# The up product of a decoder layer: eight pairs of output tiles by seven products of quarters, and low parts by adding loads

## The chip, the cores and the metric

The kernel runs on one core of one Trainium2 chip. The metric is device time in microseconds for one execution of the program, median of several runs. All arithmetic is on fp32 data. The matrix engine (TensorE, PE in the profile) works on operands rounded to fp32r, so the kernel splits each fp32 matrix into a high part (the rounded value) and a low part (what is left over), and forms each product as three: high by high, high by low, low by high.

## The reference

One decoder layer with 512 tokens (T), width 1024 (D) and feed-forward width 2816. The mixers ahead of the feed-forward part are not touched. What matters here:

```python
def conv_ffn(h, w_up, conv_w, conv_b, w_down):
    up = h @ w_up                              # 512 x 1024 by 1024 x 5632
    padded = jnp.pad(up, ((0, 0), (CONV_WIDTH - 1, 0), (0, 0)))
    conv = conv_b + conv_w[0] * padded[:, 0:T]
    for i in range(1, CONV_WIDTH):
        conv = conv + conv_w[i] * padded[:, i:i + T]
    gate, val = jnp.split(conv, 2, axis=-1)
    return (jax.nn.gelu(gate, approximate=True) * val) @ w_down
...
        h = rmsnorm(x, norm_ffn_pre[l])
        f = conv_ffn(h, ffn_w_up[l], ffn_conv_w[l], ffn_conv_b[l], ffn_w_down[l])
        x = x + rmsnorm(f, norm_ffn_post[l])
```

## The kernel before

**The up product.** The output of `h @ w_up` is kept with channels on the partitions: 44 tiles of 128 channels by 512 tokens, each in one bank of PSUM (the matrix engine's accumulators). They come in 22 pairs (`NF`): tile 2n is the gate and tile 2n+1 the value of pair n. The right operand is `h2h`/`h2l`, the high and low part of the normalised activations: 128 partitions, 8 chunks (`KC`) of the width, 512 tokens. The left operand is one weight tile of 128 x 1024 for each output tile, 512 KB in fp32, which holds 8 chunks of 128 x 128. `up_mm` walks over the 8 chunks, and `mm3` (L110 to L114) issues the three matmuls of a chunk, 128 x 512 each: 24 matmuls a tile, 48 a pair. The first two pairs (`FIRST`) are done in halves of 256 tokens, since their operand is finished in halves. The other 20 run one after the other in the loop over `j`.

**The weights.** `prefetch` goes through a fixed list (`weight_order`) two tiles ahead of use (`AHEAD`). For each tile `load_raw` loads the fp32 weights from HBM into `raw` (two buffers, issued on the SP queue), ScalarE casts them into `whi` (L70), and VectorE subtracts to get `wlo` (L71). `whi` and `wlo` have four buffers each. A buffer is written again only when the last matmul that reads it is done, and an engine works through its own instructions strictly in the program's order.

**Behind each pair.** `up_finish` runs the three taps of the convolution on both tiles (`conv`: one ScalarE activation, L837, and two VectorE operations, L838 and L840, which read PSUM), the gelu on ScalarE (L852) and the product on VectorE. The down product that follows is itself made of seven products of quarters (the list `steps`) in place of eight; its left operands are sums and differences of halves of the activations, which `up_finish` forms at once for each pair of pairs (`y7`, `a2`, `ay`; L864 is one such difference of 128 x 256).

**The down product.** It runs through seven steps of six chunks of weights. The weights of a step are made from those of the step before in the six `chain` buffers: either a plain load on SP, or a load on the POOL queue that adds what it reads to what the buffer holds (`accum_op=ALU.add`, L883). `w_prepare` splits a chunk (L70 and L71 again) and then issues the load for the next step; `l_prepare` splits the left operand of a step, 4 chunks at a time; `q_mm` does the matmuls (128 x 512), and `combine`, `lower_token` and `upper_token` put the steps' results together, normalise and store.

Of the kernel before, what the change touches and what calls it, by code (L numbers as in the profile page):

```python
# [14 lines left out]
P = 128  # L15
# [9 lines left out]
TH = T // 2  # L25
LEVELS = (64, 32, 16, 8, 4, 2, 1)
# [10 lines left out]
def weight_order():  # L37

    o = [("t", T_SK), ("t", T_GQ)] + [("v", k) for k in range(8)]
    o += [("t", T_GQ + 1)] + [("t", T_GK + i) for i in range(2)] + [("t", T_R + i) for i in range(4)]  # L40
    for br in (1, 0, 2):
        for m in range(8):
            if br == 1 and m == 6:
                o += [("t", T_PU + g) for g in range(4)]
            if m % 2 == 0:
                o.append(("b", br, m // 2))
            o.append(("t", T_GATE + GATE_OF[br] * 8 + m))
    o += [("o", k) for k in range(4)] + [("u", i) for i in range(2 * NF)]
    return o
# [3 lines left out]
def kernel(ctx: ExitStack, tc: tile.TileContext, x, xT, w_first, w_tiles, w_v, w_br, w_out, w_up, w_down,  # L53
# [775 lines left out]
    with tc.tile_pool(name="fp", bufs=1) as fp:  # L829
        y7 = fp.tile([P, 2, NH, TH], F32R, tag="y7", name="y7")  # L830
        a2 = fp.tile([P, 2, NH, TH], F32, tag="a2", name="a2")
        ay = fp.tile([P, 4, NH, TH], F32, tag="ay", name="ay")
        ch = [fp.tile([P, 2 * T], F32, tag=f"ch{p}", name=f"chain{p}") for p in range(4)]
        def conv(ps, i, keep=False):
            t0 = (fp.tile([P, T], F32, tag="tk", name="tk", bufs=2) if keep else
                  fp.tile([P, T], F32, tag="t0", name="t0", bufs=3))
# [7 lines left out]
        kept = {}  # L844

        def up_finish(n, pg, pv):


            i = n // 2
            tg = conv(pg, 2 * n, n % 2 == 0)  # L850
            tv = conv(pv, 2 * n + 1)
            nc.scalar.activation(tg, tg, AF.Gelu_apprx_tanh)  # L852
            if n % 2 == 0:
                nc.vector.tensor_mul(tg, tg, tv)
                nc.vector.tensor_sub(tv[:, :TH], tg[:, TH:], tg[:, :TH])
                nc.scalar.copy(y7[:, 0, i, :], tv[:, :TH])
                nc.scalar.copy(ay[:, 2, i, :], tg[:, :TH])
                nc.vector.tensor_sub(y7[:, 1, i, :], tv[:, :TH], y7[:, 0, i, :].bitcast(F32))
                kept[i] = tg
            else:  # L860
                t0 = kept.pop(i)
                nc.vector.tensor_mul(a2[:, :, i, :], tg.rearrange("p (h t) -> p h t", h=2),
                                     tv.rearrange("p (h t) -> p h t", h=2))
                nc.vector.tensor_sub(ay[:, 0, i, :], t0[:, TH:], a2[:, 1, i, :])  # L864
                nc.vector.tensor_sub(ay[:, 1, i, :], t0[:, :TH], ay[:, 0, i, :])
                nc.vector.tensor_sub(ay[:, 3, i, :], a2[:, 0, i, :], ay[:, 1, i, :])
# [3 lines left out]
        steps = ((None, (1, 1), True), (ay[:, 2], (0, 0), False), (ay[:, 0], (0, 1), True), (ay[:, 1], (1, 1), True),  # L870
                 (a2[:, 1], (1, 0), True), (ay[:, 3], (1, 1), False), (a2[:, 0], (1, 0), False))
# [18 lines left out]
        def w_prepare(upto):  # L890
            while len(ready) < min(upto, len(todo)):
                s, p = todo[len(ready)]
                k0, k1 = pairs[p]
                hi, lo = new_w()
# [5 lines left out]
        for i in range(2 * FIRST):  # L900
            up_mm(pf[i], up_first[i], slice(256, 512))
        for j in range(FIRST):
            up_finish(j, pf[2 * j], pf[2 * j + 1])
        for j in range(FIRST, NF):
            pp = []
            for i in (2 * j, 2 * j + 1):
                w = weight("u", i)
                ps = psm.tile([P, T], F32, tag="mm", name=f"up{i}")
                up_mm(ps, w, slice(0, T))
                pp.append(ps)  # L910
            if j == NF - 5:
                for p in range(4):
                    chain_load(0, p)
            if j == NF - 1:
                w_prepare(2)
                ch += [wp.tile([P, 2 * T], F32, tag="raw", name=f"chain{p}", bufs=2) for p in (4, 5)]
                for p in (4, 5):
                    chain_load(0, p)
            up_finish(j, *pp)

        lh = hp.tile([P, 2, 2, 4, TH], F32R, tag="hhi", name="lhs")
        cb = hp.tile([P, 4, 2, T], F32, tag="hlo", name="comb")
        gpost = cb.rearrange("p i b c -> p i (b c)")[:, 3, :]
        nc.gpsimd.dma_start(gpost, g_ffn_post.partition_broadcast(P))
        nc.gpsimd.tensor_scalar(gpost, gpost, -0.5, None, op0=ALU.mult)
        left = {}

        def l_split(s, g):
# [3 lines left out]
            nc.scalar.copy(lh[:, h, 0, :n, :], src)  # L932
            nc.vector.tensor_sub(lh[:, h, 1, :n, :], src, lh[:, h, 0, :n, :].bitcast(F32))
            left[s, g] = h

        lgroups = [(s, g) for s in range(1, len(steps)) for g in range(len(groups))]
# [4 lines left out]

        def lhs(s, k, part, tb):
            tk = slice(tb * P, (tb + 1) * P)
            if s == 0:
                return y7[:, part, k, tk]
            return lh[:, left[s, k // 4], part, k % 4, tk]
# [73 lines left out]
        for s in range(len(steps)):  # L1020
            whole = len(pairs) if s < len(steps) - 1 else 3
            for p in range(whole):
                w_prepare(s * len(pairs) + p + (3 if whole == len(pairs) else 4))
                if p % 2 == 0:
                    l_prepare((s - 1) * len(groups) + p // 2 + 2 if s else 2)
# [103 lines left out]
```

## Time and profile before

| | |
|---|---|
| Time, median of 3 runs | 780.96 us (779.97 to 781.41) |
| The profiled execution's own time | 781.12 us |
| Its span, first to last instruction | 779.3 us |
| Mean granted clock of TensorE | 0.998 of full speed |
| Up product whole tiles, matmuls 128x512 | 960 (three rows of 320, 389 ns mean duration) |
| HBM read, written | 89.84 MB, 2.10 MB |

The page gives one execution. Engines are named PE (TensorE's matmuls), PEld (its weight loads, which overlap the matmuls), DVE (VectorE), ACT (ScalarE), POOL (GpSimd) and SP (which only issues loads and stores here). A duration of a matmul in the trace reaches from its start until its result is written, and matmuls overlap; so their price is read from the distance of their starts and not from their durations. A load is listed with the time from its issue until its last byte has landed. A stretch is given as from:to in us, with busy time and number of instructions of each engine.

### The profile page before, as it was taken

The numbers are of one execution on the slowest core, as the hardware profiler recorded it, in microseconds if no ns is written. First come the engines' busy times: TensorE is split into PE (matmuls) and PEld (weight loads), VectorE is DVE, ScalarE is ACT, GpSimd is POOL, SyncE is SP. The second block draws the span as 40 slices with busy tenths as digits, with TensorE's granted clock in tenths as the row PEclk, the third lists the DMA queues.
The fourth block names the chain that finished last, engine by engine and source line by source line (L and its number), as shares of the span: only waits on it lengthen the run. The fifth ranks groups of instructions, "written<-read, shape, count | busy, mean of one in ns | idle before, by whom it ended". The sixth has DMA issues, their size and how long they took to land.

```text
span 779.3 us, 9734 instructions
## 1 busy us (share of the span) xinstructions
PE 770.3 (99%) x3686; PEld 638.9 (82%) x3686; DVE 514.5 (66%) x784; ACT 356.9 (46%) x583; POOL 55.1 (7%) x70
## 2 busy tenths in 40 slices
PE   9999999999999999999999999999999999999996
PEld 8899776888886888888888988888888888888885
DVE  5564688378696555654648557766666766766896
ACT  6554554482233442423535434434344343565582
POOL 0100000002513000000000100000000000233000
PEclk9999999999999999999999999999999999999999
DMA  8524212122133212232351483322323225499761
GB/s 309 193 89 146 71 57 79 55 85 105 54 104 127 70 66 86 105 102 87 131 221 54 139 211 111 109 108 82 109 84 105 105 84 135 130 185 193 200 212 54
DMA packets 28526, 92.56 MB, mean 119 GB/s; under 512 B 3392, under 2 KB 3664, under 8 KB 28480
## 3 DMA queue, kind: packets, MB, share of 16 engines
q1 hardware_dynamic: 24048, 77.83, 29.0%
q0 software_dynamic: 4288, 14.11, 9.1%
q8 instruction: 29, 0.48, 0.2%
q14 instruction: 17, 0.14, 0.1%
q10 hardware_dynamic: 144, 0.00, 0.0%
HBM read 89.84 MB, written 2.10 MB: 118 GB/s over the span
## 4 chain that ended last, share of the span: by engine, by line
PE 97%; DMA 1%; DVE 1%; ACT 0%; issue 0%; DVEq 0%; ACTq 0%
PE up L113 10%; PE up L112 10%; PE up L114 10%; PE pj L112 9%; PE pj L113 9%; PE pj L114 8%; PE q L962 4%; PE q L963 4%; PE q L964 4%; PE py L112 3%; PE py L114 3%; PE py L113 3%; PE pq L206 3%; PE pz L749 2%; PE pz L751 2%; PE pz L750 2%
## 5 line engine op out<-in xcount | busy, mean ns | idle before, releaser
L71 DVE TENSOR_TENSOR wlo<-raw,whi 128x1024 fp32r<-128x1024 f32 (+1 forms) x105 | 125.3, 1196 | 112.3 <-ACT whi L70 112.3
L70 ACT CAST whi<-raw 128x1024 fp32r<-128x1024 f32 (+1 forms) x105 | 107.5, 1025 | 182.9 <-PE pj L113 89.1
L112 PE MATMUL up<-h_hi,whi 128*128 128x512 f32 (+1 forms) x384 | 143.8, 375 | 0.0
L113 PE MATMUL up<-h_lo,whi 128*128 128x512 f32 (+1 forms) x384 | 142.7, 372 | 0.0
L114 PE MATMUL up<-h_hi,wlo 128*128 128x512 f32 (+1 forms) x384 | 142.5, 371 | 0.0
L112 PE MATMUL pj<-h_hi,whi 128*128 128x512 f32 x296 | 120.5, 407 | 0.0
L113 PE MATMUL pj<-h_lo,whi 128*128 128x512 f32 x296 | 116.1, 392 | 0.0
L114 PE MATMUL pj<-h_hi,wlo 128*128 128x512 f32 x296 | 115.8, 391 | 0.0
L113 PEld LDWEIGHTS up<-h_lo,whi 128*128 128x128 f32 x384 | 72.3, 188 | 12.5
L114 PEld LDWEIGHTS up<-h_hi,wlo 128*128 128x128 f32 x384 | 72.3, 188 | 12.5
L112 PEld LDWEIGHTS up<-h_hi,whi 128*128 128x128 f32 x384 | 72.2, 188 | 12.6
L112 PEld LDWEIGHTS pj<-h_hi,whi 128*128 128x128 f32 x296 | 55.7, 188 | 15.9 <-issue 3.4
L114 PEld LDWEIGHTS pj<-h_hi,wlo 128*128 128x128 f32 x296 | 55.6, 188 | 12.1 <-issue 0.2
L113 PEld LDWEIGHTS pj<-h_lo,whi 128*128 128x128 f32 x296 | 55.8, 188 | 10.5 <-issue 1.0
L71 DVE TENSOR_TENSOR wlo<-chain,whi 128x1024 fp32r<-128x1024 f32 (+1 forms) x42 | 47.3, 1132 | 19.9 <-ACT whi L70 19.9
L70 ACT CAST whi<-chain 128x1024 fp32r<-128x1024 f32 (+1 forms) x42 | 41.1, 981 | 29.6 <-PE q L964 22.8
L883 POOL DMA_DIRECT2D chain<-in_w_down_dram x24 | 21.0, 876 | 438.6 <-ACT tk L837 201.3
L962 PE MATMUL q<-whi,lhs 128*128 128x512 f32 x132 | 51.3, 389 | 0.0
L963 PE MATMUL q<-wlo,lhs 128*128 128x512 f32 x132 | 51.3, 389 | 0.0
L964 PE MATMUL q<-whi,lhs 128*128 128x512 f32 x132 | 51.3, 389 | 0.0
L674 DVE TENSOR_TENSOR g<-pj,rstd_b 128x512 f32<-128x512 f32 x24 | 16.4, 688 | 27.4 <-PE pj L114 27.3
L964 PEld LDWEIGHTS q<-whi,lhs 128*128 128x128 f32 x132 | 24.8, 188 | 5.2
(308 smaller groups left out, 1264.4 us busy)
## 6 DMA issues: line engine op xcount, KB each, us to landing
raw<-in_w_up_dram SPq DMA_DIRECT2D x44, 512.0 KB, 3.2
raw<-in_w_tiles_dram SPq DMA_DIRECT2D x37, 512.0 KB, 3.2
chain<-in_w_down_dram SPq DMA_DIRECT2D x20, 512.0 KB, 4.4
chain<-in_w_down_dram POOLq DMA_DIRECT2D x20, 512.0 KB, 7.5
raw<-in_w_br_dram SPq DMA_DIRECT2D x12, 512.0 KB, 3.3
raw<-in_w_out_dram SPq DMA_DIRECT2D x8, 512.0 KB, 3.2
raw<-in_w_v_dram SPq DMA_DIRECT2D x8, 328.0 KB, 2.9
xT<-in_xT_dram SPq DMA_DIRECT2D x8, 256.0 KB, 5.0
```

The lines of the kernel that those rows point to most:

```text
L70: nc.scalar.copy(hi[:, c], raw[:, c])
L71: nc.vector.tensor_sub(lo[:, c], raw[:, c], hi[:, c].bitcast(F32))
L112: nc.tensor.matmul(ps, lh, rh, start=first, stop=False)
L113: nc.tensor.matmul(ps, lh, rl, start=False, stop=False)
L114: nc.tensor.matmul(ps, ll, rh, start=False, stop=last)
L206: nc.tensor.matmul(pq[i], w[:, kc, i * P : (i + 1) * P], h[:, kc, :], start=kc == 0 and n == 0, stop=kc == KC - 1 and n == 2)
L674: nc.vector.tensor_mul(g1, gates.pop((br, m)), rstd_b)
L749: nc.tensor.matmul(pz[t][n], mh[:, kc % 4, tk], wh[:, ns], start=kc == 0, stop=False)
L883: nc.gpsimd.dma_start(c, w_down[kh, nh, :, k, :], accum_op=ALU.add)
L962: nc.tensor.matmul(ps, hi, wh[:, c], start=k == 0 and not last, stop=False, skip_group_check=last)
L963: nc.tensor.matmul(ps, hi, wl[:, c], start=False, stop=False, skip_group_check=last)
L964: nc.tensor.matmul(ps, lo, wh[:, c], start=False, stop=k == NH - 1, skip_group_check=last)
```

## The change

Pairs n = 5, 7, ..., 19 (`SEVEN`) are computed by seven products of quarters. The weights of such a pair are seen as a 2 x 2 block matrix (two halves of the width, two tiles of channels), the activations as 2 x 2 as well (two halves of the width, two halves of the tokens). Seven products of sums and differences of the quarters, four chunks deep and 256 tokens wide, replace the eight that the plain way amounts to. One product is 4 chunks by 3 terms, 12 matmuls of 128x256 (`part_mm`). `up_seven` interleaves the seven products with the plain pair n+1, whose tiles 2n+2 and 2n+3 are called A and B in the prediction. A "double pair" is the two together; the order of work in it is quarter b11, 2 chunks of A, p3, 3 chunks of A, p2, 3 chunks of A, b21, 2 chunks of B, p1, 3 chunks of B, p4, 3 chunks of B, b22.

Four operands `ys0` to `ys3` are formed once from the activations (`y_steps`, while the pairs 2 to 4 run). The weights' sums are formed for each double pair: `sra` is a plain load of 512 KB, `s1` two plain loads of 256 KB and two adding loads on top (`s_load`, issued at the end of p4's preparation for the next double pair; one buffer), `s2` comes from additions on VectorE. The weight slots become one ring of eight half tiles: a plain tile takes two, a quarter one (`slots`, `place`, `free`). `fill` prepares as far ahead as the ring has room, in the order of use. For plain tiles from number 10 on, the low part is no longer a VectorE subtraction: ScalarE writes `-raw`, rounded like the high part, into the low buffer, and a load on POOL adds the fp32 weights from HBM on top (L939, L940). Results of the seven products are kept as copies of PSUM on ScalarE (`keep`, L1080) and put together on VectorE.

For the down product `up_finish` now stores only products and one difference (`act`); two of the other differences move into `l_split` (steps 3 and 5), step 0's operand is split there too, and the `chain` buffers 0 to 3 take the place of `ys0` and `ys1` once the last double pair is done.

```diff
+SEVEN = (5, 7, 9, 11, 13, 15, 17, 19)
...
-    o += [("o", k) for k in range(4)] + [("u", i) for i in range(2 * NF)]
+    o += [("o", k) for k in range(4)] + [("u", i) for i in range(2 * FIRST)]
...
+        def slots(n):
+            if n == 2 and slot["n"] % 2:
+                slot["n"] += 1
+            i = slot["n"] % 8
+            slot["n"] += n
+            c = slice(i % 2 * T, (i % 2 + n) * T)
+            return wt[i // 2][0][:, c], wt[i // 2][1][:, c]
...
             if n % 2 == 0:
...
+                nc.vector.tensor_sub(act[:, 4, i, :], act[:, 1, i, :], act[:, 0, i, :])
             else:
...
+                nc.vector.tensor_sub(act[:, 1, i, :], act[:, 1, i, :], act[:, 3, i, :])
...
+        def s_load(n):
+            qt["a"] = f4(f"sra{n}", "sra")
+            nc.sync.dma_start(qt["a"], w_up[2 * n])
+            qt["s1"] = f4(f"s1_{n}", "sm1")
+            nc.sync.dma_start(qt["s1"][:, :T], w_up[2 * n, :, :T])
+            nc.sync.dma_start(qt["s1"][:, T:], w_up[2 * n + 1, :, T:])
+            for h in range(2):
+                nc.gpsimd.dma_start(qt["s1"][:, h * T : (h + 1) * T], w_up[2 * n + 1, :, :T], accum_op=ALU.add)
+
+        def half(src):
+            hi, lo = slots(1)
+            nc.scalar.copy(hi, src)
+            nc.vector.tensor_sub(lo, src, hi.bitcast(F32))
+            return hi, lo
+
+        def prep(item):
+            if item[0] == "t":
+                hi, lo = slots(2)
+                raw = load_raw(w_up[item[1]])
+                nc.scalar.copy(hi, raw)
+                if True and item[1] >= 2 * SEVEN[0]:
+                    nc.scalar.activation(lo, raw, AF.Copy, scale=-1.0)
+                    nc.gpsimd.dma_start(lo, w_up[item[1]], accum_op=ALU.add)
+                else:
+                    nc.vector.tensor_sub(lo, raw, hi.bitcast(F32))
+                return hi, lo
...
+            if q == "p2":
+                s2 = qt["s2"] = f4(f"s2_{n}", "sm2")
+                nc.vector.tensor_add(s2[:, :T], a[:, :T], s1[:, T:])
+                return half(s2[:, :T])
...
+            if q == "p4":
+                s2 = qt["s2"]
+                nc.vector.tensor_add(s2[:, T:], s2[:, :T], a[:, T:])
+                r = half(s2[:, T:])
+                later = [m for m in SEVEN if m > n]
+                if later:
+                    s_load(later[0])
+                return r
...
+        def fill():
+            while done["i"] < len(items):
...
+                if at + size - min(place.values(), default=at) > 8 or (it[0] == "s" and not qt):
+                    break
+                place[it] = at
+                got_w[it] = prep(it)
+                done["i"] += 1
...
+            if s == 3:
+                nc.vector.tensor_sub(src, src, act[:, 1, k0:k1, :])
+            if s == 5:
+                nc.vector.tensor_sub(src, act[:, 2, k0:k1, :], act[:, 0, k0:k1, :])
...
+        def part_mm(ps, w, r, first):
+            for kc in range(4):
+                c = slice(kc * P, (kc + 1) * P)
+                terms = ((w[0], r[0]), (w[0], r[1]), (w[1], r[0]))
+                for t, (x, y) in enumerate(terms):
+                    nc.tensor.matmul(ps[:, :TH], x[:, c], y[:, kc, :], start=first and kc == 0 and t == 0,
+                                     stop=kc == 3 and t == 2, skip_group_check=not first)
...
+            b11, p3 = up_weight("s", n, "b11"), up_weight("s", n, "p3")
+            part_mm(bx, b11, hq(0, 0), True)
+            free("s", n, "b11")
+            q1 = keep("q1", bx)
+            wa = up_weight("t", 2 * n + 2)
+            whole_mm(pn[0], wa, range(0, 2))
+            part_mm(by, p3, yq(0), True)
...
```

TensorE where output tile `up19` ends and `up20` begins, before the change: rows of one kind, tile after tile (`whi` and `wlo` are the weight buffers with their running numbers).

```order
L112 MATMUL up19_4371<-h2_hi_3100,whi_4291 128x512
L113 MATMUL up19_4371<-h2_lo_3101,whi_4291 128x512
L114 MATMUL up19_4371<-h2_hi_3100,wlo_4292 128x512
L112 MATMUL up20_4415<-h2_hi_3100,whi_4336 128x512
L113 MATMUL up20_4415<-h2_lo_3101,whi_4336 128x512
L114 MATMUL up20_4415<-h2_hi_3100,wlo_4337 128x512
```

So every low part is read right behind the first two matmuls of its tile.

The same tile of output, `up20`, as tile A of the double pair n = 9, after the change, from the first of its own rows: `uy_9` and `ux_9` are accumulators of the quarter products, `ys0` and `ys1` the new operands.

```order
L113 MATMUL up20_4463<-h2_hi_3100,whi_3670 128x512
L114 MATMUL up20_4463<-h2_lo_3101,whi_3670 128x512
L1059 MATMUL uy_9_4461<-ys0_3672,whi_3668 128x256 x2
L1059 MATMUL uy_9_4461<-ys0_3672,wlo_3669 128x256
L1059 MATMUL uy_9_4461<-ys0_3672,whi_3668 128x256 x2
L1059 MATMUL uy_9_4461<-ys0_3672,wlo_3669 128x256
L1059 MATMUL uy_9_4461<-ys0_3672,whi_3668 128x256 x2
L1059 MATMUL uy_9_4461<-ys0_3672,wlo_3669 128x256
L1059 MATMUL uy_9_4461<-ys0_3672,whi_3668 128x256 x2
L1059 MATMUL uy_9_4461<-ys0_3672,wlo_3669 128x256
L1059 MATMUL ux_9_4460<-ys1_3673,whi_3664 128x256 x2
L1059 MATMUL ux_9_4460<-ys1_3673,wlo_3665 128x256
```

Between the second matmul of `up20` and its third, the one that reads the low part `wlo`, now stand two groups of quarter matmuls: p3's twelve, and six of the twelve of p2, whose first half stands ahead of it in this row.

ScalarE at the same place of the program. Before the change, casts of the weights (L70), starts of the convolution (L837) and gelus (L852) take turns:

```order
L70 CAST whi_4411<-raw_4409 128x1024
L837 ACTIVATE t0_4396<-up18_4340,small_sb_86 128x512
L852 ACTIVATE t0_4396<-t0_4396 128x512
L70 CAST whi_4442<-raw_4440 128x1024
L837 ACTIVATE t0_4400<-up19_4371,small_sb_86 128x512
L70 CAST whi_4487<-raw_4485 128x1024
```

After it, around the preparation of `up20` (its `raw` is number 4414, its slots `whi_3670` and `wlo_3671`, which tile B of the double pair before, `up17`, holds until its last matmul). L929 is a cast of a quarter, L937 that of a plain tile, L939 its negated copy, L1080 a copy out of PSUM, L883 a start of the convolution, L896 a gelu:

```order
L929 CAST whi_3664<-s2_9_4419 128x512
L929 CAST whi_3668<-s2_9_4419 128x512
L929 CAST whi_3664<-sra9_4311 128x512
L883 ACTIVATE t0_4438<-ua_7_4256,small_sb_86 128x512
L937 CAST whi_3670<-raw_4414 128x1024
L939 ACTIVATE wlo_3671<-raw_4414 128x1024
L1115 ACTIVATE ub_7_4257<-ux_7_4251 128x256
L896 ACTIVATE t0_4438<-t0_4438 128x512
L883 ACTIVATE t0_4442<-ub_7_4257,small_sb_86 128x512
L883 ACTIVATE t0_4449<-up16_4254,small_sb_86 128x512
L1080 ACTIVATE q1_4479<-ux_9_4460 128x256
L937 CAST whi_3666<-raw_4481 128x1024
```

All casts of the sums for n = 9 and the convolution's start on the sum `ua_7` now stand ahead of the cast of `up20`'s weights, and the gelu and three more starts of the convolution behind it; the next plain tile's cast (`raw_4481`) is queued behind those.

More of the change, by code (lines that the diff above doesn't have):

```diff
@@ L829 @@
     with tc.tile_pool(name="fp", bufs=1) as fp:
[L830 to L836, printed above, removed]
+        act = fp.tile([P, 5, NH, TH], F32, tag="act", name="act")
@@ new lines, with f4 @@
+        wt = [new_w() for _ in range(4)]
+        slot = {"n": 0}
+        def slots(n):
[5 more added lines that the diff above has]
+            return wt[i // 2][0][:, c], wt[i // 2][1][:, c]
+        def f4(name, tag):
+            return fp.tile([P, 1024], F32, tag=tag, name=name)
+        ys = [fp.tile([P, 2, 4, TH], F32R, tag=f"ys{i}", name=f"ys{i}") for i in range(4)]
@@ new lines, with up_weight @@
+        place = {}
+        def fill():
+            while done["i"] < len(items):
+                it = items[done["i"]]
+                size = 2 if it[0] == "t" else 1
+                at = slot["n"] + (size == 2 and slot["n"] % 2)
+                if at + size - min(place.values(), default=at) > 8 or (it[0] == "s" and not qt):
[3 more added lines that the diff above has]
+                done["i"] += 1
+        def up_weight(*item):
+            assert items[done["taken"]] == item, (items[done["taken"]], item)
+            done["taken"] += 1
+            fill()
+            return got_w[item]
@@ L872, with free @@
+        def free(*item):
+            del place[item]
+        steps = ((act[:, 4], (1, 1), True), (act[:, 0], (0, 0), False), (act[:, 1], (0, 1), True),
+                 (act[:, 0], (1, 1), True), (act[:, 3], (1, 0), True), (act[:, 1], (1, 1), False),
+                 (act[:, 2], (1, 0), False))
         pairs = tuple((k, min(k + 2, NH)) for k in range(0, NH, 2))
@@ L898, in w_prepare @@
                     chain_load(s + 1, p)
[L900 to L925, printed above, removed]
         left = {}
@@ new lines @@
+        for i in range(2 * FIRST):
+            up_mm(pf[i], up_first[i], slice(256, 512))
+        for j in range(FIRST):
+            up_finish(j, pf[2 * j], pf[2 * j + 1])
+        yst = y_steps()
+        n = FIRST
+        while n < NF:
+            if n in SEVEN:
+                us, pn = up_seven(n)
+                up_finish(n, *us)
+                up_finish(n + 1, *pn)
+                n += 2
+                if n - 2 == SEVEN[-1]:
+                    c0 = fp.tile([P, 2, 2 * T], F32, tag="ys0", name="chain01")
+                    c1 = fp.tile([P, 2, 2 * T], F32, tag="ys1", name="chain23")
+                    ch = [c0[:, 0, :], c0[:, 1, :], c1[:, 0, :], c1[:, 1, :]]
+                    for p in range(4):
+                        chain_load(0, p)
+                continue
+            pp = up_std(n)
+            if n == NF - 1:
+                lh = [fp.tile([P, 2, 4, TH], F32R, tag=f"ys{i}", name=f"lhs{i}") for i in (2, 3)]
+                l_prepare(2)
+                w_prepare(2)
+                ch += [wp.tile([P, 2 * T], F32, tag="raw", name=f"chain{p}", bufs=2) for p in (4, 5)]
+                for p in (4, 5):
+                    chain_load(0, p)
+            up_finish(n, *pp)
+            for _ in range(3):
+                next(yst, None)
+            n += 1
+            if n == SEVEN[0] - 1:
+                for _ in yst:
+                    pass
+                s_load(SEVEN[0])
```

137 lines of the change are left out of this document (113 added, 24 removed).

## The prediction, as it was made before the changed kernel was run

> **What bounds the kernel now.** I read the page first, then busy time by stretch, then the matmuls one by one. From the page (span, part 1, and part 4, the chain that ended last):
>
> ```profile
> span 779.3 us, 9734 instructions
> ...
> PE 770.3 (99%) x3686; PEld 638.9 (82%) x3686; DVE 514.5 (66%) x784; ACT 356.9 (46%) x583; POOL 55.1 (7%) x70
> ...
> PE 97%; DMA 1%; DVE 1%; ACT 0%; issue 0%; DVEq 0%; ACTq 0%
> ```
>
> TensorE holds 97% of the chain: a matmul removed is time won, and a pause put into its row is time lost. By stretch (length, then busy us of PE, PEld, DVE, ACT, POOL, granted clock, DMA share, GB/s):
>
> ```profile
> 483.00:657.00 174.00, 174.00 (x769) 144.10 (x768) 114.59 (x155) 72.21 (x97) 1.73 (x2) 1.00 0.30 102
> ...
> 549.00:571.00 22.00, 22.00 (x99) 18.22 (x98) 14.05 (x19) 9.25 (x14) 0.00 (x0) 1.00 0.28 96
> ...
> 683.00:698.00 15.00, 15.00 (x68) 12.43 (x67) 8.86 (x9) 8.59 (x11) 4.85 (x6) 1.00 1.05 189
> 698.00:713.00 15.00, 15.00 (x67) 12.41 (x67) 10.09 (x10) 9.45 (x12) 5.28 (x7) 1.00 1.03 189
> 743.00:758.00 15.00, 15.00 (x68) 12.43 (x67) 15.00 (x28) 12.51 (x21) 0.00 (x0) 1.00 0.68 217
> ```
>
> The first row is exactly 16 of the up pairs, those that become the eight double pairs (a pair of seven products with a plain pair woven in): 768 matmuls in 174.0 us, 0.2266 us each, 10.88 us a pair, without a gap. VectorE and ScalarE are two thirds and two fifths busy there, POOL not at all.
>
> **What is removed.** The trace already has matmuls 256 wide, in the first pairs (start, duration):
>
> ```profile
> 440.45 0.28 PE L114 MATMUL up<-h_hi,wlo 128*128 128x256 f32 x1
> ...
> 443.45 0.28 PE L112 MATMUL up<-h_hi,whi 128*128 128x256 f32 x1
> ...
> 448.49 0.19 PEld L113 LDWEIGHTS up<-h_lo,whi 128*128 128x128 f32 x1
> ```
>
> From the first start to the last are 25 steps: 0.120 us each, though each has its own weight load of 0.19 us, which overlaps. Half the width costs 0.120, not 0.113. A pair of seven products is 7 x 12 = 84 of these, 10.08 us, in place of 10.88. The saving is 0.80 us a pair, **6.4 us** in all, and a double pair is 48 x 0.2266 + 10.08 = 20.96 us of TensorE.
>
> **What is added beside it.** Durations by line and shape (busy us, mean ns):
>
> ```profile
> L71 DVE TENSOR_TENSOR wlo<-raw,whi 128x1024 fp32r<-128x1024 f32 x97 | 118.7, 1226 | 103.8 <-ACT whi L70 103.8
> ...
> L70 ACT CAST whi<-raw 128x1024 fp32r<-128x1024 f32 x97 | 101.6, 1049 | 171.4 <-PE pj L113 87.2 <-PE up L113 40.0 <-DMA raw<-in_w_up_dram 17.3
> ...
> L837 ACT ACTIVATE t<-up,small_sb 128x512 f32<-128x512 f32 x33 | 25.6, 776 | 0.0
> ...
> L840 DVE SCALAR_TENSOR_TENSOR t<-up,small_sb,t 128x510 f32<-128x510 f32 x33 | 24.7, 748 | 1.1
> ...
> L852 ACT ACTIVATE t<-t 128x512 f32<-128x512 f32 x11 | 6.9, 632 | 21.2 <-DVE t L840 21.2
> ...
> L396 ACT COPY s<-sc 128x256 f32<-128x256 f32 x16 | 5.1, 373 | 0.2
> ...
> L71 DVE TENSOR_TENSOR wlo<-chain,whi 128x512 fp32r<-128x512 f32 x7 | 4.8, 686 | 0.0
> ...
> L864 DVE TENSOR_TENSOR ay<-tk,a 128x256 f32<-128x256 f32 x11 | 4.7, 424 | 0.3
> ...
> L70 ACT CAST whi<-chain 128x512 fp32r<-128x512 f32 x7 | 4.3, 621 | 1.4 <-PE q L964 1.1
> ```
>
> ScalarE in a double pair: seven half casts 4.3, two full casts and two negated copies (nearest row: the full cast) 4.2, five copies out of PSUM 1.9, four convolution starts 3.1, two gelus 1.3: 14.8 of 20.96 us. VectorE: seven half low parts 4.8, two half sums 1.4, three 256-wide sums 1.3, eight convolution taps 6.0, two products 1.4, two differences 0.8: 15.7. Both fit as totals. The order decides, so I followed two loops through it. In T I count from the start of the last matmul of tile B, the second plain tile of a double pair.
>
> *Loop A: the ring of weight slots.* The next tile A (up20 in the rows shown) goes into the slots of this tile B (up17). Its cast can't start until tile B is done, and its low part now takes a negated copy and an adding load after that.
>
> ```profile
> 564.10 0.39 PE L113 MATMUL up<-h_lo,whi 128*128 128x512 f32 x1
> ...
> 564.53 1.05 ACT L70 CAST whi<-raw 128x1024 fp32r<-128x1024 f32 x1 [3.71 <-PE up L113]
> 565.49 0.77 ACT L837 ACTIVATE tk<-up,small_sb 128x512 f32<-128x512 f32 x1
> ```
>
> The last matmul that reads the old high part starts 0.23 before T and lasts 0.39; the cast follows 0.04 us after such an end, so at T+0.20; the next ScalarE instruction starts 0.96 after a cast of 1.05. Cast and copy end at T+2.2, and POOL issues at T+2.3. Landing times, from issue, of plain loads (SP) and adding loads (POOL), then single adding loads at 655.0 and 720.3 us, and the queues between 679 and 721 us:
>
> ```profile
> raw<-in_w_up_dram SPq DMA_DIRECT2D x44, 512.0 KB, 3.2
> ...
> chain<-in_w_down_dram POOLq DMA_DIRECT2D x20, 512.0 KB, 7.5
> ...
> chain<-in_w_down_dram SPq DMA_DIRECT2D x4, 256.0 KB, 3.6
> chain<-in_w_down_dram POOLq DMA_DIRECT2D x4, 256.0 KB, 7.9
> ```
>
> ```profile
> L883 POOL DMA_DIRECT2D chain<-in_w_down_dram x1: 863/863/863, 655.0 to 655.0; - x1
> ...
> DMA to landing us min/median/max: 5.2/5.2/5.2
> ```
>
> ```profile
> L883 POOL DMA_DIRECT2D chain<-in_w_down_dram x1: 875/875/875, 720.3 to 720.3; - x1
> ...
> DMA to landing us min/median/max: 8.4/8.4/8.4
> ```
>
> ```profile
> q0 software_dynamic: 2201, 7.51, 98.9%
> q1 hardware_dynamic: 135, 0.23, 1.5%
> ```
>
> The quietest adding load takes 5.2 us. Where they follow one another, adding loads alone fill the 16 DMA engines (7.51 MB in 42 us, 98.9%) and take up to 8.4. In the new stage they are 1.5 MB of a double pair, about 8 us of full DMA by that rate, so nearer to the quiet row; I take 6.2, between 5.2 and 8.4. The low part is there at T+2.3+6.2+0.1 = T+8.6. In TensorE's row stand before the matmul that wants it: the rest of tile B's last matmul 0.23, twenty-four quarter matmuls 2.88, two of tile A 0.45, eighteen more quarters 2.16: T+5.7. **TensorE waits 2.9 us** (1.9 at 5.2, 5.1 at 8.4, nothing at 3.3), and every later matmul is queued behind. A double pair takes 23.9.
>
> The Trainium skill's page "DMA: Bandwidth & Descriptors", section "Anatomy of one DMA — SWDGE (gpsimd) path", fits a DMA as 2.0 us plus bytes over 436 GB/s. For 512 KB that gives an estimate of 3.2 us, by which loop A wouldn't wait and the sum would end near the second rival. The plain loads' row (3.2) agrees with it; the adding rows (5.2 to 8.4) don't, so I go by those.
>
> *Loop B: the sums of weights.* The one buffer for the quarter sums is loaded again only after quarter p1's low part has been taken. From one tile A cast to the next, in ScalarE's row: four full instructions 4.2, three 256-wide copies 1.1, two gelus 1.3, three convolution starts 2.3, the half cast of p1 0.6, less twelve overlaps of 0.08: 8.6. Then p1's low part 0.7 with hand-offs 0.1; two loads of 256 KB, 3.6 and 0.2 for the second; two adding loads, the second issued 0.95 later and landing after 4.6 (bounds: 3.9, which is 5.2 less half of the 2.7 us that 512 KB took at the full rate, and 7.9). Then, with each waiting for the one before: half sum, two half low parts, a 256-wide difference, the other half sum, p4's half cast and low part, a 256-wide sum and the convolution's start, 5.6 less overlaps 0.2. Only then comes the next cast in ScalarE's row. 8.6+0.8+3.8+0.95+4.6+5.4 = **24.2 us** (23.5 to 27.5). Loop B is the longer by a hair, and I take 24.2 as the period of a double pair.
>
> *The rest.* The first double pair: four new operands of h are formed on VectorE, twelve operations of about 1.2 us, in the idle third of the 45 us before it. The first sums then land at about 485 us, when TensorE wants them; I take 0.8 (0 to 3). The last tile, 43, has tile B's slots too: low part at T+8.6, wanted after twelve quarters, tile 42 and two matmuls, T+7.6: 1.1 (0 to 3). Down product: six differences and three more low parts, 10 us of VectorE. The differences stand in its first three steps, where 5 to 6 us of each 15 are free (683 to 713 us by stretch), and the order of the full last steps (743 to 758 us, VectorE busy throughout) is unchanged: nothing; without that cover up to 7 us. The down product's first loads move from far ahead to about 24 us ahead of need: nothing.
>
> **Sum.** 20.96 + 0.8 + 7 x 24.2 = 191.2 against 174.0: +17.2, and 1.1: +18.3. On the profiled execution, 781.1 us: **799.4**. The median shown is 780.96, 0.02% away.
>
> **Rivals.** *The adding loads crowd each other*, as at 720 us. Loop A 26.1, loop B 27.5: 20.96 + 2 + 7 x 27.5 = 215.5 and 3 at tile 43, +44: 825. For it: three of them a double pair beside 2.3 MB of plain loads. Against: they are spread over 24 us.
>
> *The adding loads land like plain ones, and it ends faster.* Place: the low part of tile A and the sums. 512 KB in 3.2 us ends loop A's wait. With 2.5 for 256 KB, loaded or added (3.2 less the 0.7 that a quarter MB takes at plain speed), loop B is 8.6+0.8+2.7+0.95+2.5+5.4 = 21.0. Then 20.96 + 7 x 21.0 = 168, -6: 775. It decides at a period of 21.8, where 20.96 + 7 x 21.8 = 174. Against: no adding load of 24 took under 5.2, and no 256 KB load with others beside it 2.5.
>
> *The clock drops in the pauses.* At the end TensorE stands still from 772.8 us:
>
> ```profile
> 772.70:776.00 3.30, 0.10 (x1) 0.00 (x0) 2.59 (x8) 0.98 (x3) 0.00 (x0) 1.00 0.43 159
> 776.00:779.00 3.00, 0.00 (x0) 0.00 (x0) 0.33 (x1) 0.00 (x0) 0.00 (x0) 0.55 0.47 175
> ```
>
> It kept its clock for 3.2 us and had 0.55 on average after. Pauses of 2.9 to 3.5 us are at that edge. If each cost 3 us at 0.55, that is 1.4 us, seven times 10: 809. The Trainium skill's "TensorE: Matmul & The Clock Gate", section "HAM oscillation — how this bites in real kernels", names idle gaps over about 3.4 us as what halves the clock, and speaks against this change. These two rows agree with it.
>
> *It isn't what it says*: quarter matmuls slower among wide ones than among their like. At the 0.19 us of their weight loads 84 take 15.8, 40 us in all: 840. The rows at 440 us speak against it.
>
> **How the numbers follow.** Forecast 0.64, crowding 0.14, clock 0.08, faster 0.09, slow quarters 0.02, and 0.03 for a mix that cancels. Below the forecast stands loop A alone at 5.2: 20.96 + 7 x 22.9 = 181, 788; the range begins a little under it and ends between forecast and crowding: **785 to 820**. Within 0.2% is about what a measurement of this kernel can't tell from none. Faster 0.09, same 0.03, slower 0.88.
>
> **What would show it.** In the changed profile: a wait of TensorE of 2 to 5 us once in a double pair, before the matmul of tile A that reads its low part, ended by the adding load; adding loads of 512 KB landing after 5 to 8 us; tile A's cast following a convolution's start at once; quarter matmuls 0.120 us apart; no wait in the down product. A double pair near 21 us, or adding loads landing in under 4, would make the prediction wrong.

## The result, and the profile after

| | before | after |
|---|---|---|
| Time, median (lowest to highest) | 781.05 us (779.97 to 781.41) | **840.13 us** (839.00 to 843.67) |
| Ratio | | 1.0766, 95% interval 1.0753 to 1.0779 |
| Profiled execution, own time / span | 781.12 / 779.3 us | 839.0 / 837.2 us |

Slower, as forecast, but by 59 us where 18 were forecast, and outside the range that ended at 820. The page of the profile after (span; part 1; the granted clock by slices; the chain that ended last):

```profile
span 837.2 us, 10523 instructions
...
PE 788.4 (94%) x3974; PEld 661.5 (79%) x3974; DVE 534.4 (64%) x834; ACT 397.1 (47%) x666; POOL 85.7 (10%) x104
...
PEclk9999999999999999999999999989999989899999
...
PE 72%; DMA 12%; issue 6%; ACT 5%; DVE 3%; POOL 1%; DVEq 0%; POOLq 0%; ACTq 0%
```

TensorE carried 97% of the chain before and carries 72% now; transfers have 12%, and VectorE and ScalarE, which had next to nothing, 8%. What TensorE waits for (total us, times, longest; `issue` means that the profile shows nothing it waited for):

```profile
PE up L115 <- DMA wlo<-in_w_up_dram: 26.3, 10, 3.8
PE ux L1059 <- ACT q L1080: 5.4, 6, 1.2
PE uy L1059 <- issue: 4.8, 1, 4.8
PE ux L1059 <- ACT u L1080: 2.1, 1, 2.1
PE up L113 <- ACT whi L937: 1.3, 2, 0.8
```

The first row is the wait that the prediction named: the matmul of a plain tile that reads its low part, behind an adding load. The 4.8 us of the third row end at 490.91, 0.7 us after the first sums' loads have landed. But a wait shows only what was late, not what sets the pace. So I cut the stage by the starts of TensorE's pieces of work: 483.12 us the first double pair, 514.79 the second, 706.47 the last pair (tiles 42 and 43), 725.53 the down product.

| Stretch | before, same work | forecast | measured |
|---|---|---|---|
| First double pair | 21.76 | 20.96 + 0.8 | 31.7 |
| Seven double pairs, each | 21.76 | 24.2 | 27.4 (191.7 / 7) |
| Tiles 42 and 43 | 10.88 | 10.88 + 1.1 | 19.1 |

The differences to the forecast are 9.9, 22.3 and 7.1 us: 39.3 of the 39.6 from 799.4 to the profiled execution's 839.0. One period of loop B, from tile A's cast (the rows of four engines, n = 15; the first number is the start, the second the length). ScalarE:

```profile
597.37 1.03 ACT L937 CAST whi<-raw 128x1024 fp32r<-128x1024 f32 x1
...
605.03 0.63 ACT L929 CAST whi<-s 128x512 fp32r<-128x512 f32 x1
...
619.27 0.63 ACT L929 CAST whi<-s 128x512 fp32r<-128x512 f32 x1 [4.73 <-DMA s<-in_w_up_dram]
...
624.63 1.03 ACT L937 CAST whi<-raw 128x1024 fp32r<-128x1024 f32 x1
```

The loads, on SP and POOL, and the first sum on VectorE:

```profile
606.56 0.33 SPq L922 DMA_DIRECT2D s<-in_w_up_dram  x1
606.94 0.48 SPq L923 DMA_DIRECT2D s<-in_w_up_dram  x1
```

```profile
603.98 0.88 POOL L940 DMA_DIRECT2D wlo<-in_w_up_dram  x1 [3.45 <-ACT n L1080]
612.13 0.88 POOL L925 DMA_DIRECT2D s<-in_w_up_dram  x1 [7.27 <-DVE wlo L930]
```

```profile
605.85 0.68 DVE L930 TENSOR_TENSOR wlo<-s,whi 128x512 fp32r<-128x512 f32 x1
...
619.27 0.69 DVE L952 TENSOR_TENSOR s<-sra,s 128x512 f32<-128x512 f32 x1 [3.26 <-DMA s<-in_w_up_dram]
```

Tile A's cast at 597.37; p1's low part 605.85 to 606.53; then at once s1's plain loads, 606.56; the adding loads at 612.13; the sums at 619.27, when VectorE had stood idle for 3.3 us and ScalarE for 4.7; the next tile A's cast at 624.63. The pieces add up to the period, 27.26 us, and no matmul is among them. The same cut for each double pair:

| Up to tile A's cast of n = | 9 | 11 | 13 | 15 | 17 | 19 | mean | forecast |
|---|---|---|---|---|---|---|---|---|
| cast to s1's plain loads (engines) | 9.17 | 9.34 | 9.18 | 9.19 | 9.18 | 9.18 | 9.21 | 9.4 |
| plain loads to adding loads | 5.63 | 6.30 | 6.44 | 5.57 | 6.47 | 6.97 | 6.23 | 3.8 |
| adding loads to sums | 6.11 | 8.09 | 5.93 | 7.14 | 6.12 | 5.54 | 6.49 | 5.55 |
| sums to the next cast (engines) | 5.36 | 5.35 | 5.36 | 5.36 | 5.36 | 5.36 | 5.36 | 5.4 |
| period | 26.3 | 29.1 | 26.9 | 27.3 | 27.1 | 27.1 | 27.3 | 24.2 |

(Column 15 is the period that ends with the cast at 624.63. A column for n = 7 would begin with tile 12's cast at 472.22, ahead of the stage, and is left out.) The engines' parts are constant and as forecast; the loads are not. What was beside them, from the DMA issues (count, size, median us to landing):

```profile
raw<-in_w_up_dram SPq DMA_DIRECT2D x28, 512.0 KB, 4.0
...
wlo<-in_w_up_dram POOLq DMA_DIRECT2D x18, 512.0 KB, 7.4
...
s<-in_w_up_dram SPq DMA_DIRECT2D x16, 256.0 KB, 6.1
s<-in_w_up_dram POOLq DMA_DIRECT2D x16, 256.0 KB, 5.3
```

A plain load of 256 KB takes 6.1 us, longer than one of 512 KB. Tile B's adding load is issued 2.6 to 2.7 us ahead of it (603.98 in the period shown) in each of these periods.

The clock dropped too (stretches around the wait in n = 9: length, PE, PEld, DVE, ACT, POOL, granted clock, DMA share, GB/s):

```profile
544.50:545.85 1.35, 0.12 (x1) 0.00 (x1) 0.95 (x2) 1.35 (x4) 0.04 (x1) 1.00 1.04 237
545.85:546.83 0.98, 0.98 (x6) 0.77 (x6) 0.98 (x2) 0.98 (x2) 0.00 (x0) 1.00 0.82 117
546.83:548.50 1.67, 0.00 (x0) 0.00 (x0) 1.64 (x4) 1.62 (x3) 0.51 (x1) 1.00 0.98 194
548.50:549.40 0.90, 0.00 (x0) 0.00 (x0) 0.24 (x2) 0.90 (x3) 0.36 (x1) 0.66 0.83 241
549.40:555.30 5.90, 5.89 (x14) 4.64 (x15) 2.95 (x5) 1.04 (x2) 0.00 (x0) 0.50 0.89 199
```

A pause of 1.4 us, a second of work, a pause of 2.6, and then about 6 us of full work at half the clock.

### The profile page after: what moved, and what is told of

Read it like the earlier page. It is cut to its first block, busy times and chain, and to the rows that moved or that the text cites. A ratio compares the mean times of both kernels' runs of the same rounds, so it can differ in the third digit from the quotient of the medians.

```text
span 837.2 us, 10523 instructions
## 1 busy us (share of the span) xinstructions
PE 788.4 (94%) x3974; PEld 661.5 (79%) x3974; DVE 534.4 (64%) x834; ACT 397.1 (47%) x666; POOL 85.7 (10%) x104
## 4 chain that ended last, share of the span: by engine, by line
PE 72%; DMA 12%; issue 6%; ACT 5%; DVE 3%; POOL 1%; DVEq 0%; POOLq 0%; ACTq 0%
PE pj L113 8%; DMA s<-in_w_up_dram 8%; PE pj L114 8%; PE pj L115 8%; PE q L1179 4%; PE q L1177 4%; PE q L1178 4%; PE up L115 3%; PE up L114 3%; PE up L113 3%; DMA wlo<-in_w_up_dram 3%; PE py L113 3%; PE py L114 3%; PE py L115 3%; PE pq L207 3%
## 5 line engine op out<-in xcount | busy, mean ns | idle before, releaser
L71 ACT CAST whi<-raw 128x1024 fp32r<-128x1024 f32 (+1 forms) x65 | 65.5, 1010 | 132.3 <-PE pj L114 88.4
L115 PE MATMUL up<-h_hi,wlo 128*128 128x512 f32 (+1 forms) x256 | 100.0, 391 | 26.3 <-DMA wlo<-in_w_up_dram 26.3
L72 DVE TENSOR_TENSOR wlo<-raw,whi 128x1024 fp32r<-128x1024 f32 (+1 forms) x65 | 76.3, 1179 | 52.0 <-ACT whi L71 51.9
L113 PE MATMUL up<-h_hi,whi 128*128 128x512 f32 (+1 forms) x256 | 100.3, 393 | 1.3 <-ACT whi L937 1.3
L114 PE MATMUL up<-h_lo,whi 128*128 128x512 f32 (+1 forms) x256 | 99.1, 388 | 0.0
L115 PEld LDWEIGHTS up<-h_hi,wlo 128*128 128x128 f32 x256 | 52.1, 203 | 37.7 <-DMA wlo<-in_w_up_dram 29.0
L113 PEld LDWEIGHTS up<-h_hi,whi 128*128 128x128 f32 x256 | 51.7, 203 | 8.8 <-ACT whi L937 1.7
L114 PEld LDWEIGHTS up<-h_lo,whi 128*128 128x128 f32 x256 | 51.8, 202 | 7.4
L940 POOL DMA_DIRECT2D wlo<-in_w_up_dram x18 | 16.5, 918 | 352.0 <-ACT wlo L939 233.4
L929 ACT CAST whi<-s 128x512 fp32r<-128x512 f32 x32 | 19.6, 619 | 62.3 <-DMA s<-in_w_up_dram 51.5
L1059 PE MATMUL ux<-ys,whi 128*128 128x256 f32 x192 | 36.7, 288 | 7.5 <-ACT q L1080 5.4
```

The source lines that it names most:

```text
L71: nc.scalar.copy(hi[:, c], raw[:, c])
L72: nc.vector.tensor_sub(lo[:, c], raw[:, c], hi[:, c].bitcast(F32))
L113: nc.tensor.matmul(ps, lh, rh, start=first, stop=False)
L114: nc.tensor.matmul(ps, lh, rl, start=False, stop=False)
L115: nc.tensor.matmul(ps, ll, rh, start=False, stop=last)
L929: nc.scalar.copy(hi, src)
```

## The experiments

Three theories. **1**: the loop through the one s1 buffer (loop B) sets the period, and its loads take longer than forecast. **2**: the wait for the low parts' adding loads (loop A) does. **3**: the clock does. Each run below is the changed kernel with the edit shown, unless it says otherwise. A time without a ratio is that of one execution; four of the changed kernel lay between 839.0 and 843.67.

### Two buffers for the sums

```diff
-            qt["s1"] = f4(f"s1_{n}", "sm1")
+            qt["s1"] = f4(f"s1_{n}", "sm1", 2)
...
-                s2 = qt["s2"] = f4(f"s2_{n}", "sm2")
-                nc.vector.tensor_add(s2[:, :T], a[:, :T], s1[:, T:])
+                nc.vector.tensor_add(s1[:, T:], a[:, :T], s1[:, T:])
```

> The changed kernel, but the quarter sums s1 have two buffers (the room comes from making the other two sums in place), so that a double pair's sums are loaded while the pair before still uses its own. Same loads, same arithmetic. Theory 1 (the period of 27.4 us is the loop through the one s1 buffer: p1's low part, two plain loads, two adding loads, sums, half casts, tile A's cast): the period falls to the other loop, tile A's low part by an adding load of about 6.8 us after a cast that waits for tile B's slots, 20.96 + 3.5 = 24.5 us; time 840 - 7 x 2.9 = 820 us. Theory 2 (the period is set by the adding loads of the low parts alone): 840 us, no change. Theory 3 (the clock that drops in the pauses sets it): 840 us or a little less, with the clock still dropping.

Measured 817.07 us (the kernel before beside it: 780.9). Three of its double pairs (same columns as above):

```profile
558.20:583.20 25.00, 22.89 (x134) 20.33 (x133) 14.55 (x25) 13.19 (x23) 3.52 (x4) 0.93 0.64 158
583.20:606.80 23.60, 21.29 (x133) 19.11 (x132) 14.63 (x25) 13.19 (x23) 3.52 (x4) 1.00 0.70 167
606.80:630.20 23.40, 21.30 (x133) 19.12 (x132) 14.59 (x25) 13.20 (x23) 3.52 (x4) 1.00 0.70 169
```

The same loads and sums, only asked for a double pair earlier, and the period falls from 27.4 to between 23.4 and 25.1, but for one: n = 9 still took 27.5, with the clock at 0.88. So loop B was the bound, theory 2 alone is out, and loop A by itself gives 23.5 at the full clock (23.9 forecast). Theory 3, which expected 840 or a little less here, is 23 us off, though the clock still drops in three double pairs. Here, where TensorE is in the loop, the clock counts: a double pair with one short drop (0.93) takes some 1.5 us more than one without.

### The sums on VectorE

```diff
-            nc.sync.dma_start(qt["s1"][:, :T], w_up[2 * n, :, :T])
-            nc.sync.dma_start(qt["s1"][:, T:], w_up[2 * n + 1, :, T:])
-            for h in range(2):
-                nc.gpsimd.dma_start(qt["s1"][:, h * T : (h + 1) * T], w_up[2 * n + 1, :, :T], accum_op=ALU.add)
+            nc.sync.dma_start(qt["s1"], w_up[2 * n + 1])
+            nc.vector.tensor_add(qt["s1"][:, T:], qt["s1"][:, T:], qt["s1"][:, :T])
+            nc.vector.tensor_add(qt["s1"][:, :T], qt["s1"][:, :T], qt["a"][:, :T])
```

> The changed kernel, but s1 is one plain load of 512 KB and two VectorE additions in place (0.69 us each) instead of two plain loads and two adding loads of 256 KB; still one buffer. Theory 1: the loop through s1 becomes 8.5 + 4.5 + 1.4 + 5.4 = 19.8 us, so tile A's low part decides at about 24.5: 820 us, and some 3 us less in the first double pair: 817. Theory 2: 840 us. Theory 3: 840 us or a little less.

Measured 815.49 us. One buffer is kept, but without the adding loads in it the loop is short enough; the waits for low parts stay (25.1 us in all).

### The low parts on VectorE

```diff
-                if True and item[1] >= 2 * SEVEN[0]:
+                if False:
```

> The changed kernel, but the low parts of the plain tiles are VectorE subtractions again (no negated copies on ScalarE, no adding loads of 512 KB). The sums still come by adding loads in one buffer. Theory 1: the loop through s1 loses two negated copies (1.9 us) and its loads lose what crowds them: 6.6 + 0.1 + 4.5 + 6.5 + 5.4 = 23.1 us, up to 25 if the two subtractions of 1.2 us hold the convolution up; 840 - 7 x 3.5 - 5 at tiles 42 and 43 = 810 us (800 to 822). Theory 2: no wait is left, period near 21: 840 - 7 x 6.4 - 7 = 788 us. Theory 3 as theory 2, since the pauses go.

Measured 807.85 us: theory 1's figure (810), not the 788 of the others. Every wait for a low part's load is gone, and the period is still 24.6 to 26.7 from the third double pair on, since loop B stands: 9.63 (VectorE's subtractions hold p1's low part up as much as the copies did), 3.7 to 5.6, 6, 5.35. Its loads:

```profile
s<-in_w_up_dram SPq DMA_DIRECT2D x16, 256.0 KB, 3.7
s<-in_w_up_dram POOLq DMA_DIRECT2D x16, 256.0 KB, 5.0
```

Without the low parts' adding loads the plain 256 KB take 3.7 us, as in the kernel before (3.6).

### Which adding load crowds them

The low part of tile B alone (odd tiles) on VectorE:

```diff
-                if True and item[1] >= 2 * SEVEN[0]:
+                if item[1] % 2 == 0 and item[1] >= 2 * SEVEN[0]:
```

> The changed kernel with the low parts of the odd plain tiles (tile B of each double pair, and 43) by VectorE subtraction; tile A and tile 42 keep the adding load. In the changed kernel tile B's adding load of 512 KB is issued at about 604.0 and lands at about 611, and the two plain loads of s1, issued at 606.6, land only with it (5.6 to 7 us). If that one crowds them (theory 1a), they now take 3.6 to 4; ScalarE's and VectorE's part from tile A's cast to them is 9.2 less one negated copy or more; so the loop through s1 is about 8 + 4 + 6 + 5.4 = 23.4 and tile A's low part decides at 24.5: 840 - 7 x 2.9 - 2 = 818 us. If what crowds them is not tile B's adding load: 5.6 to 7 us as before, period 26.5, 834 us.

Then that of tile A alone (even tiles; the same line with `== 1`):

> The other half: the even plain tiles (tile A of each double pair, and 42) by VectorE subtraction, tile B and 43 by the adding load. Theory 1a: the plain loads of s1 still land late, 5.6 to 7 us; loop through s1 about 9 + 6 + 6 + 5.4 = 26.4; no wait for an adding load is left in front of tile A, but TensorE waits for tile A's cast instead, behind the sums; the first double pair's sums are not crowded by tile A's load any more (-4) and tile 42 has no adding load behind the down product's (-4): 840 - 7 x 1 - 8 = 825 us. If tile A's wait were what sets the period: 20.96 to 22 in place of 27.4 us, 790 to 795 us.

Measured 821.01 and 829.11 us. The loads with tile B on VectorE:

```profile
wlo<-in_w_up_dram POOLq DMA_DIRECT2D x9, 512.0 KB, 6.8
s<-in_w_up_dram SPq DMA_DIRECT2D x16, 256.0 KB, 3.8
```

and with tile A on VectorE:

```profile
wlo<-in_w_up_dram POOLq DMA_DIRECT2D x9, 512.0 KB, 8.1
s<-in_w_up_dram SPq DMA_DIRECT2D x16, 256.0 KB, 6.0
```

3.8 against 6.0: of the adding loads it is tile B's that holds s1's plain loads (plain loads of `raw` stand beside them in both runs). With tile A's wait for a load gone (the second of the two) the period is still 25.1 to 26.8. In the first the period came out at 24.6 to 27.4, above the 24.5 expected: the engines' part did not shorten (9.66, VectorE's subtraction in the copies' place), and the sums' adding loads took 6.0 to 8.3.

### The two ends

Tiles 12, 13, 42 and 43 on VectorE:

```diff
-                if True and item[1] >= 2 * SEVEN[0]:
+                if 14 <= item[1] < 42:
```

> The changed kernel with four low parts by VectorE subtraction: tiles 12 and 13 (plain tiles of the first double pair) and 42 and 43 (the last two). Theory: the first double pair's 32 us are due to tile 12's adding load, issued 0.5 us ahead of the sums' plain loads, which then take 7.4 us in place of 3.7; and the 8.2 us at tiles 42 and 43 are due to the down product's adding loads that stand ahead of theirs on the POOL queue. So the first double pair falls to about 26 us as in the third run, the last two tiles to 10.9, the six in between stay: 840 - 6 - 8 = 826 us (823 to 830). If both are after-effects of what stands before and behind: 838 or more.

Measured 825.25 us. The first double pair takes 23.9 us (26 expected), tiles 42 and 43 take 10.91, and the periods between stay at 26.8 to 28.7. In the changed kernel the first double pair's loads were issued in this order, POOL and then SP:

```profile
476.15 0.94 POOL L940 DMA_DIRECT2D wlo<-in_w_up_dram  x1 [233.41 <-ACT wlo L939]
```

```profile
476.67 0.33 SPq L922 DMA_DIRECT2D s<-in_w_up_dram  x1
477.05 0.42 SPq L923 DMA_DIRECT2D s<-in_w_up_dram  x1
```

Tile 12's adding load stands half a microsecond ahead, and the plain loads took until 484.1, 7.4 us, in place of 3.2 in this run. At the other end the POOL queue of the changed kernel:

```profile
699.42 0.88 POOL L1009 DMA_DIRECT2D chain<-in_w_down_dram  x1 [3.48 <-DMA chain<-in_w_down_dram]
699.96 1.24 POOL L940 DMA_DIRECT2D wlo<-in_w_up_dram  x1
704.74 0.88 POOL L1009 DMA_DIRECT2D chain<-in_w_down_dram  x1 [3.54 <-DMA chain<-in_w_down_dram]
```

Tile 42's low part is issued behind an adding load of the down product that itself waited 3.5 us, shares its transfer, and lands 11 us after its issue; TensorE waits 3.77 us for it.

### Filling the pauses

Two tries to hold the clock up with matmuls that change no result:

```diff
             whole_mm(pn[0], wa, range(0, 2))
             part_mm(by, p3, yq(0), True)
...
+            for _ in range(12):
+                nc.tensor.matmul(bz, h2h[:, 0, :P], h2h[:, 0, :], start=True, stop=True)
```

> The changed kernel with 12 matmuls of 128x512 more in each double pair, behind quarter p3, into an accumulator that is overwritten later; they use data that is always there and fill the pause before tile A's low part (2.8 us of work). They change no result. Theory 1: the loop through s1 has no matmul in it, so the period stays at 27.4; the clock stays up in the double pairs and it gains nothing there: 840 us within 4. Theory 3: each double pair loses 2.5 to 3 us at the half clock, so keeping the clock up brings 840 - 7 x 2.5 = 822 us. If TensorE were the bound, the added work would cost 8 x 2.8 = 22 us: 862.

and 24 of them ahead of tile A's first matmul:

> As the fourth run, with 24 matmuls of 128x512 (5.4 us) put ahead of tile A's first, where nothing can be drawn in front of them. A double pair has 20.96 + 5.4 = 26.4 us of work, still under the period of 27.4. Theory 1: the loop through s1 has no matmul in it; the pause shrinks to about 1 us, the clock stays up, and the time stays 840 us (836 to 846). Theory 3 (the half clock sets the period): 840 - 7 x 2.5 = 822 us or less. If every matmul counted: 840 + 8 x 5.4 = 883.

848.16 and 850.21 us, both above the 840 that theory 1 expected, and neither settles anything. In the first, nine of the twelve came to stand behind the wait and not in it, the clock still dropped, and loop B's last part grew from 5.4 to between 5.7 and 8.6 us. In the second the clock stayed up in the later pairs and the period stayed at 26.5 to 27.7, but the added work held up ScalarE's copies out of PSUM, and loop B's first part grew from 9.2 to about 12 us while its plain loads fell to 3.5 to 4.6; TensorE's own work was 26.4 us by then. That is another loop of the same length by chance. Against theory 3 stand the table of the loop, which has no matmul in it, and the run with two buffers, and not these two.

### The low parts alone, in the kernel before

```diff
-            loaded[k] = load_w(src, VC if k[0] == "v" else 1024)
+            if k[0] == "u" and k[1] >= 10:
+                raw = load_raw(src)
+                hi, lo = new_w()
+                nc.scalar.copy(hi, raw)
+                nc.scalar.activation(lo, raw, AF.Copy, scale=-1.0)
+                nc.gpsimd.dma_start(lo, src, accum_op=ALU.add)
+                loaded[k] = hi, lo
+            else:
+                loaded[k] = load_w(src, VC if k[0] == "v" else 1024)
```

> The kernel before with one thing of the change alone: from tile 10 on the low part of every up weight is a negated copy on ScalarE and an adding load of 512 KB (34 of them); no products of quarters. Here a tile's buffers come free three tiles (16 us) ahead of need, and cast, copy and adding load of 7.5 take some 10. Theory 1: hidden: 781 us within 2. Rival (adding loads beside the plain ones cost by themselves, by traffic or by late landing): 34 x 0.5 us or more, above 795.

781.59 us, ratio 1.0008 (0.9999 to 1.0017): 34 adding loads cost nothing there that can be told from noise. They are no faster:

```profile
raw<-in_w_up_dram SPq DMA_DIRECT2D x44, 512.0 KB, 6.1
wlo<-in_w_up_dram POOLq DMA_DIRECT2D x34, 512.0 KB, 7.8
```

The crowding is all there (plain loads 6.1 in place of 3.2), but an adding load is issued 13.8 us, two and a half tiles, ahead of the matmul that reads its low part, and lands some 6 us ahead of it (from tile 16 on).

### Both parts relieved

The sums and the low parts on VectorE (the second and the third edit together):

> The changed kernel without any adding load in the up product: low parts of the plain tiles by VectorE subtraction and s1 by one plain load and two additions on VectorE. Theory 1: both loops fall under TensorE's own 20.96 us: tile A's low part at T + 0.2 + 1.05 + 1.2 + 0.1 = T + 2.6 against a need at T + 5.7, the loop through s1 6.6 + 0.8 + 3.5 + 1.4 + 5.4 = 17.7, up to 20 with two subtractions more in the way. So the saving of 6.4 us comes out but for some 1.5 us in the first double pair: 776 us (774 to 779), faster than the kernel before. Rival: VectorE, 19.5 of 20.96 us busy, is now the bound through the order of its work, and each double pair still waits 1 us or more: 783 us or above.

776.09 us, ratio 0.9930 (0.9913 to 0.9946). And two buffers with the low parts on VectorE (the first and the third edit):

> The changed kernel with two buffers for s1 (as in the first run) and low parts of the plain tiles by VectorE subtraction (as in the third); the sums still come by adding loads of 256 KB, now a whole double pair ahead. Theory 1: neither loop is left; the first double pair still waits up to 2 us for its sums: 777 us (775 to 781). If the adding loads as such were what slows the chip, whatever waits for them, it would stay above 790.

775.53 us. The same kernel again, the median of five executions:

> The sixth run's kernel, timed against the kernel before: two buffers for s1, low parts by VectorE subtraction. Expected 775.5 us (774.5 to 776.5), faster by 0.6 to 0.8%: the saving of 6.4 us less 8 x 0.12 us that a double pair takes over 20.96.

**774.91 us, ratio 0.9924 (0.9911 to 0.9938)**: faster than the kernel before. What TensorE waits for in it, the whole list, and a stretch in its double pairs:

```profile
PE warm L183 <- POOL ones L167: 1.0, 1, 1.0
PE go L611 <- DVE y_pool_lo L331: 0.9, 1, 0.9
```

```profile
526.00:547.00 21.00, 21.00 (x134) 18.99 (x133) 16.30 (x27) 11.52 (x21) 1.78 (x2) 1.00 0.49 139
```

No wait is left in the up product, the clock is full, and a double pair takes 21.08 us (502.88 to 523.96, and so on). Sixteen adding loads of 256 KB are still in it; the rival that adding loads as such slow the chip is out.

## Why the prediction went wrong, point by point

- **The saving of 6.4 us: right.** 0.120 us a quarter matmul, 20.96 a double pair; measured 21.08 where nothing waits, so 8 x 0.12 less: 5.4; the three timings without waits gained 5.0 to 6.0. The rival of slow quarter matmuls, whose 840 is the very time measured, is out: they start 0.119 to 0.120 us apart in the changed kernel as well wherever the clock is full. Its 840 was a wrong sum besides: 8 x (15.8 - 10.88) are 40 us on the time before, 821, and with 26.7 us of TensorE's own work in a double pair both loops would have been covered. A time that agrees proves no mechanism.
- **Loop A: right, but not the bound.** 23.9 forecast, 23.5 measured with the other loop taken away. The rival in which adding loads land like plain ones is out: they took 7.4 us in the median. The Trainium skill's page "DMA: Bandwidth & Descriptors", section "Anatomy of one DMA — SWDGE (gpsimd) path", gives by its fit an estimate of 3.2 us for a DMA of 512 KB; the runs don't bear it out for adding loads.
- **Loop B named as the longer one: right; its loads mis-sized.** The step that failed is "two loads of 256 KB, 3.6 and 0.2 for the second", and after it 0.95 + 4.6 for the adding ones. They took 6.23 and 6.49 us, 12.7 in place of 9.35, while the engines took 14.6 in place of 14.8; that is the whole of 27.3 less 24.2, about 22 us if all seven pairs are counted alike. The price of 3.6 is right for the load alone (3.7 without the low parts' loads). It went wrong because tile B's adding load is always in flight then. The 0.9 us more of the adding ones are not explained: without any low part's load they still took about 6.

The kernel before had shown such crowding already, from 440 to 452 us, where the first loads of the down product stand beside those of the up weights:

```profile
chain<-in_w_down_dram POOLq DMA_DIRECT2D x4, 512.0 KB, 12.5
...
raw<-in_w_up_dram SPq DMA_DIRECT2D x2, 512.0 KB, 9.0
```

Plain loads of 512 KB took 8.5 and 9.5 us there, not 3.2, and the adding loads 9.0 to 15.1, beyond the 8.4 that the prediction took for the longest. (Its 2.7 us for 512 KB at the full rate is 2.9 by its own row, 7.51 MB in 42 us; that moves the lower bound of loop B from 23.5 to 23.3 and nothing else.)

- **The crowding rival: right that loads crowd each other, and near in the period** (27.5), put at 0.14. The period is partly luck: it laid the whole excess on the sums' adding loads (7.9 us), where 2.4 of the 3.4 us were in the plain ones; its loop A (26.1) did not come out, and its 825 has 1 us for the first double pair and 2 for tile 43 over the forecast, where the two ends cost 17. What I held against it, that the adding loads are spread over 24 us, was an average. The loads hang on the same chain of casts, so the same two meet in every period, 2.6 us apart.
- **The first double pair (0.8, with 3 as the bound): wrong**, 9.9 us more. I placed the sums' arrival at 485 us by undisturbed loads; tile 12's adding load was in front of them. Waits of 4.8, 1.2 and 2.1 us, and the clock behind them.
- **Tile 43 (1.1) and "the down product's first loads: nothing": wrong**, 7.1 us. The cover that I named for those loads was their own lead; I did not ask what they were moved next to. The rest of the down product was free, as said: in the run with the two ends on VectorE nothing waits there, and it takes 111.4 us from its first matmul on, as in the kernel before.
- **The clock rival: it drops, but not in the loop.** Its price in the changed kernel lies in the first pair and the last two tiles, where no run separates it from the waits; beside loop A it is 1.5 us a double pair. Its edge, a pause of some 3 us, did not come out either (last section).

## What to carry to other kernels

Follow a buffer that is filled again round its loop and price each load by what is in flight at that moment of the loop, not by a mean over the stage: loads that hang on one chain of work meet in every turn. Before moving work from an engine to the DMA, look at the lead: in a row with 13.8 us of lead the same adding loads were free; in a ring with none TensorE waited for them, and they crowded the loads of the loop that set the pace. And when an edit takes work off TensorE that everything else was hidden behind, the loops under it have to be shortened first: a second buffer for the sums and the low parts left on a VectorE that had room made of a loss of 59 us a gain of 6.

## What the runs showed that was not expected

An adding load holds back plain loads that share its time: 256 KB took 6.0 us behind one of 512 KB and 3.8 without it, and in the kernel before, with 34 adding loads, plain loads of 512 KB went from 3.2 to 6.1. The 2.2 us are less than the 2.9 that 512 KB of adding loads fill the DMA engines for by the prediction's row (7.51 MB in 42 us, an estimate), so a sharing of the engines could account for them; that is not shown.

The clock drops to 0.50 without any single long pause. Two stretches of 3.41 us in the run with two buffers, each with what follows it (columns as before):

```profile
562.52:565.93 3.41, 1.30 (x12) 1.09 (x10) 2.91 (x5) 3.41 (x7) 0.87 (x1) 1.00 0.85 169
565.93:569.34 3.41, 3.41 (x8) 2.77 (x9) 3.21 (x5) 1.02 (x2) 0.00 (x0) 0.50 0.96 208
...
661.51:664.92 3.41, 1.68 (x7) 1.42 (x8) 2.91 (x6) 1.58 (x3) 0.26 (x1) 1.00 0.83 265
664.92:668.33 3.41, 3.41 (x19) 2.90 (x19) 1.42 (x3) 1.00 (x2) 0.87 (x1) 1.00 1.04 269
```

A pause of 2.1 us (563.8 to 565.9) halved the clock, and one of 3.3 (659.95 to 663.24), which lies across the border of two such stretches, did not. In the changed kernel and the eight runs made from it whose clock drops, the clock in this stage changes only at multiples of 3.41 us from one change to the next. A full clock was halved after every such stretch in which TensorE stood idle for 0.55 of the time or more, and after none with less than 0.49 (worked out from its matmuls' rows). So what counts here is the share of idle time in a fixed stretch, not the length of one pause. In n = 9 of the changed kernel, parts of two pauses fell into one stretch. The Trainium skill's page "TensorE: Matmul & The Clock Gate", section "HAM oscillation — how this bites in real kernels", speaks of gaps over about 3.4 us; these runs don't bear that out as the threshold.
